# Moving all modulation vectors of a two-layer hybrid network onto the matrix engine

## The chip, the cores and the metric

One NeuronCore of a Trainium2 chip runs the whole network in one launch. The metric is the device time of one launch in microseconds (us), the median of several runs. TensorE multiplies matrices, VectorE (DVE), ScalarE (ACT) and GpSimd (POOL) work element by element, and SyncE (SP) only starts transfers. ACT and POOL start transfers too, each in the order of its own instructions. Every engine takes its instructions strictly in the order in which they stand, and waits on semaphores for the others.

## What is computed

Both layers begin and go on with vectors that come from a conditioning vector `c` (and, for the context rows of layer 0, from `c_ctx`):

```python
def adaln(cond, w, b):                      # w_mod: 2 layers of [1024, 6144], f32
    m = jax.nn.silu(cond) @ w + b
    return jnp.split(m[..., None, :], 6, axis=-1)

def modulate(x, g, shift, scale):
    return rmsnorm(x, g) * (1 + scale) + shift

for layer in range(2):
    sh1, sc1, gt1, sh2, sc2, gt2 = adaln(c, w_mod[layer], b_mod[layer])
    hx = modulate(x, norm_mix_g[layer], sh1, sc1)
    # layer 0: hc = modulate(ctx, ..., csh1, csc1); y = mLSTM and windowed attention of hx, hc
    # layer 1: y = gated MLP over chunks of hx (gMLP)
    x = x + gt1 * y
    x = x + gt2 * ec_moe(modulate(x, norm_ffn_g[layer], sh2, sc2), ...)   # 16 experts
```

`x` has 1024 rows of 1024, `ctx` 256 rows. One layer's weights for these vectors are 25.2 MB. Of layer 0 the first third (sh1, sc1) is needed before anything else, for `c` and for `c_ctx`; the other vectors are needed by the ends of the stages that follow.

## The kernel before, in words

The stages follow one another, by the profiled execution: the row norms and the first modulation (0 to 59 us), the transposes with the modulation and eight projections of the context (to 115), keys and values (to 160), gates and the first query (to 192), the gate arithmetic on DVE (176 to 223), the attention with the other projections filled in (223 to 625), the LSTM scan and the first routing (to 888), the first experts (to 1480), the gMLP (1488 to 2135), the second experts (to the end). Each matrix product is three fp32r products of high and low parts; the weights arrive as `wraw` (one 512 KB transfer for 128 columns), ACT casts them to `wh` (L70) and DVE or POOL subtracts to `wl` (L71).

A modulation piece is 512 of the 6144 columns; four pieces make a batch of 2048. The pieces are made in three ways:

- **Batch 0 of layer 0** (`start`, L199 to L214): eight transfers of 1 MB on SP's queue, two buffers, each followed by four matmuls with an output of two rows (c and c_ctx) by 512 columns (L201). The rows go back through DVE copies (L205) and 16 small transposes (L208). Behind them `transposed` (L161) transposes the normed rows (L167), modulates them on ACT (`hmod`, L172) and splits them into `hH` or `cH` (L175) and `hL` or `cL` (L176, every third on POOL).
- **14 pieces** (`mod_rest`, L608): POOL loads 512 KB (L617, buffers `mw`), scales them by the conditioning (L619) and sums over eight blocks of rows (L621) into a tile that it writes to memory (L625). During the attention `mod_sum` (L627) loads the tile and `mod_reduce` (L634) sums over the partitions on TensorE: four small matmuls into columns (L644), or one into a row (L638).
- **The last six pieces** (`mod_late`, L648): in the gMLP, DVE does the scaling and summing (L656, L658, L661) on tiles `s2k`, and TensorE the reduction (L644, L638). It is called behind each group of columns (L1390, L1391).

In the attention (`attention`, L376 on) each head pair and block gives scores `S` (L386 to L390), softmax pieces `ast` (L396 to L402) and `P` (L413) on DVE and ACT, transposes of P on TensorE (L415), a split into `PH` and `PL` (L417, L418) and the output `O` (L424, L425). Between them `fill` takes steps of a generator of projections (three matmuls of 512 columns a step, L228), `FILLS` says how many. The projections accumulate in the pool `pa`, two PSUM buffers `acc`, one for each half of 512 rows; each half is brought out by ACT (L444 and its like). The final order on each engine is set by a scheduler over the program, so the code's order is not quite the order of an engine.

Of the kernel before, what the change touches and what calls it, by code (L numbers as in the profile page):

```python
# [8 lines left out]
F32 = mybir.dt.float32  # L9
# [9 lines left out]
D = 1024  # L19
# [19 lines left out]
class Kernel:  # L39
# [110 lines left out]
    def normed(self, xt, sm):  # L150

        nc = self.nc
        ss = sm.tile([128, 1], F32, tag="ss", name="ss")
        junk = sm.tile([128, D], BF, tag="junk", name="junk", bufs=1)
        nc.scalar.activation(junk, xt, AF.Square, accum_out=ss)
        nc.vector.tensor_scalar(ss, ss, 1.0 / D, EPS, op0=ALU.mult, op1=ALU.add)
        r = self.rsqrt(sm, ss, 1)
        nc.vector.tensor_scalar(xt, xt, r, None, op0=ALU.mult)

    def transposed(self, xns, pp, sm, gs, sh, hH, hL, c0, f32=None):  # L160
# [3 lines left out]
        for k in range(KD):  # L164
# [3 lines left out]
            if f32 is None:  # L168
                t = sm.tile([128, 512], F32, tag="hmod", name="hmod")[:, :n]
            else:  # L170
                t = f32[:, k, c0:c0 + n]
            nc.scalar.activation(t, ps[:, :n], AF.Identity, bias=sh[:, k:k + 1], scale=gs[:, k:k + 1])  # L172
            if hH is not None:
                h = hH[:, k, c0:c0 + n]
                nc.vector.tensor_copy(h, t)  # L175
# [3 lines left out]
    def start(self):  # L179
        nc, I = self.nc, self.I  # L180
        with ExitStack() as s:
            wp = self.pool(s, "wm", bufs=2)
# [3 lines left out]
            pp = self.pool(s, "pp", bufs=2, space=PSUM)  # L186
# [6 lines left out]
            for xt in xs:  # L193
                self.normed(xt, sm)
            mod = mp.tile([2, 2048], F32, name="mod")
            sil2 = self.sil.rearrange("p (s k) -> p k s", s=2)
            for k in range(KD):
                w = wp.tile([128, 2048], F32, tag="wm", name="wm")
                nc.sync.dma_start(out=w, in_=I["w_mod"][0, k * 128:(k + 1) * 128, 0:2048])  # L199
                for j in range(4):  # L200
                    nc.tensor.matmul(mod[:, j * 512:(j + 1) * 512], sil2[:, k, :], w[:, j * 512:(j + 1) * 512],  # L201
                                     start=(k == 0), stop=(k == KD - 1))
            rows = wp.tile([2, 2048], F32, tag="wm", name="rows")
            for j in range(4):
                nc.vector.tensor_copy(rows[:, j * 512:(j + 1) * 512], mod[:, j * 512:(j + 1) * 512])  # L205
            mt = pp.tile([128, 512], F32, tag="tr", name="tr")
            for j in range(16):
                nc.tensor.transpose(mt[:, 2 * j:2 * j + 2], rows[:, j * 128:(j + 1) * 128], self.ident[0:2, 0:2])  # L208
            mc = self.cp.tile([128, 2, 16], F32, name="mc")
            nc.vector.tensor_tensor(mc, mt[:, 0:32].rearrange("p (j s) -> p s j", s=2),  # L210
                                    self.bcols[:, None, 0:16].to_broadcast([128, 2, 16]), op=ALU.add)
# [5 lines left out]
            self.transposed(xs[0:2], pp, sm, gs[:, 1, :], mc[:, 1, 0:8], self.cH, self.cL, 0)  # L217
            for g in range(2):
                self.transposed(xs[2 + 4 * g:6 + 4 * g], pp, sm, gs[:, 0, :], mc[:, 0, 0:8], self.hH, self.hL, 512 * g)
# [28 lines left out]
    def gates(self, pa, qp, hx, hc):  # L248
# [225 lines left out]
    def layer0_a(self, rings):  # L474
        nc, I = self.nc, self.I
        with ExitStack() as s:
# [87 lines left out]
            for c in range(4):  # L564
                sums = rest[cut[c - 1]:cut[c]] if c else []

                def fill(n):
                    list(itertools.islice(work, n))
                    if n == self.FILLS[2] and sums:
                        self.mod_sum(self.hxp, "hx", pt, [sums.pop(0)])  # L570
# [1074 lines left out]
```

## Time and profile before

| what | value |
|---|---|
| median of 3 runs | 2795.18 us (2794.61 to 2809.98) |
| the profiled execution: its time, its span | 2799.46 us, 2797.7 us |
| PE busy | 2499.7 us, 89% |
| DVE busy | 2061.3 us, 74% |
| ACT busy | 1530.1 us, 55% |
| POOL busy | 921.0 us, 33% |
| chain that ended last | PE 66%, DVE 8%, DMA 3%, issue 3%, ACT 2%, POOL 1% |

The span runs from the first to the last instruction of the profiled execution; the 1.8 us between it and that execution's time lie around it. That execution is 4.3 us longer than the median. The shares are averages over all stages: three quarters of the span are the experts and the gMLP, where TensorE has the work, while the first 223 us are bound by transfers, ACT and DVE in turn.

### The profile page before, as it was taken

The page shows a single profiled execution, that of the slowest core. Times are in us where ns is not written, and L with a number is a line of the kernel's source. Part 1 is how long each engine was busy: PE and PEld are TensorE (multiplying, and loading weights), DVE is VectorE, ACT ScalarE, POOL GpSimd, SP SyncE. Part 2 cuts the span into 40 slices and gives each one's busy share as a digit, 9 for nine tenths or more (in the row PEclk, how much of TensorE's full clock was granted, in tenths as well). Part 3 has the DMA queues.
Part 4 walks back from the last instruction along what each step waited for, and adds up shares of the span by engine and source line. Part 5 has one row for each costly group of instructions (what it writes and reads, how often), then busy time and mean ns, then how long its engine had stood idle before and what let it go on. Part 6 is the DMA issues. An engine that isn't in the chain of part 4 may idle for free.

```text
span 2797.7 us, 34024 instructions
## 1 busy us (share of the span) xinstructions
PE 2499.7 (89%) x12038; PEld 1999.1 (71%) x12038; DVE 2061.3 (74%) x2979; ACT 1530.1 (55%) x2262; POOL 921.0 (33%) x638
## 2 busy tenths in 40 slices
PE   6767888898895999999997999999995999999994
PEld 2656667776774788888775787888884788888773
DVE  4768798767847999999885385035505899999887
ACT  3334344445434888888864224232422788888774
POOL 0688787305531122121003324533451021321102
PEclk9978999999996999999999999999997999999997
DMA  6433434337265999999956423362334999999984
GB/s 242 134 106 114 153 123 156 105 104 269 70 230 234 362 381 382 386 383 385 364 179 208 138 83 115 92 224 76 91 121 184 365 373 388 373 389 382 357 307 150
DMA packets 246465, 648.78 MB, mean 232 GB/s; under 512 B 18572, under 2 KB 84968, under 8 KB 245270
## 3 DMA queue, kind: packets, MB, share of 16 engines
q1 hardware_dynamic: 205584, 528.44, 50.5%
q0 software_dynamic: 22096, 78.72, 10.0%
q10 hardware_dynamic: 18614, 39.44, 4.1%
q8 instruction: 95, 1.56, 0.2%
q14 instruction: 76, 0.62, 0.1%
HBM read 590.85 MB, written 53.07 MB: 230 GB/s over the span
## 4 chain that ended last, share of the span: by engine, by line
PE 66%; DVE 8%; DMA 3%; issue 3%; ACT 2%; POOL 1%; POOLq 0%; ACTq 0%; SPq 0%; DVEq 0%
PE g L1110 13%; PE u L1110 13%; PE d L1110 12%; PE acc L1461 6%; PE acc L1409 6%; PE acc L1385 5%; PE acc L781 2%; PE acc L228 2%; PE tr L1140 1%; DMA wraw<-in_gm_w_in_dram 1%; PE tr L1175 1%; PE acc L1421 1%; PE S L415 1%; PE tr L898 1%; DVE ml L71 1%
## 5 line engine op out<-in xcount | busy, mean ns | idle before, releaser
L71 DVE TENSOR_TENSOR ml<-mraw,mh 128x1024 fp32r<-128x1024 f32 x758 | 884.5, 1222 | 62.8 <-ACT mh L70 62.4
L70 ACT ACTIVATE mh<-mraw 128x1024 fp32r<-128x1024 f32 x758 | 777.3, 1064 | 143.3 <-PE g L1110 71.3
L71 POOL TENSOR_TENSOR wl<-wraw,wh 128x1024 fp32r<-128x1024 f32 (+1 forms) x133 | 257.3, 1945 | 382.8 <-ACT wh L70 378.7
L70 ACT ACTIVATE wh<-wraw 128x1024 fp32r<-128x1024 f32 (+1 forms) x163 | 143.3, 897 | 320.0 <-issue 97.1
L1190 POOL DMA_INDIRECT s_x<-xe,idx x28 | 55.5, 1982 | 662.6 <-ACT hidH L1177 421.5
L1128 POOL DMA_INDIRECT xe<-s_xr,idx x32 | 136.3, 4261 | 278.1 <-ACT mh L70 147.7
L1110 PE MATMUL d<-ml,hidH 128*128 128x512 f32 x512 | 204.5, 399 | 5.0 <-DVE ml L71 4.9
L1110 PE MATMUL g<-mh,xH 128*128 128x512 f32 x512 | 206.9, 404 | 1.4 <-ACT xH L1145 1.4
L1110 PE MATMUL d<-mh,hidH 128*128 128x512 f32 x512 | 205.2, 401 | 3.2 <-DVE o L1187 3.2
L1110 PE MATMUL g<-ml,xH 128*128 128x512 f32 x512 | 205.9, 402 | 1.4 <-DVE ml L71 1.4
L1110 PE MATMUL g<-mh,xL 128*128 128x512 f32 x512 | 205.2, 401 | 0.0
L1110 PE MATMUL u<-ml,xH 128*128 128x512 f32 x512 | 203.4, 397 | 0.2
L1110 PE MATMUL d<-mh,hidL 128*128 128x512 f32 x512 | 203.4, 397 | 0.1
L1110 PE MATMUL u<-mh,xH 128*128 128x512 f32 x512 | 202.2, 395 | 0.0
L1110 PE MATMUL u<-mh,xL 128*128 128x512 f32 x512 | 202.2, 395 | 0.0
L1385 PE MATMUL acc<-wh,h2k 128*128 128x512 f32 x512 | 167.4, 408 | 1.9 <-DVE h2k L1367 1.9
L1409 PE MATMUL acc<-h2k,wh 128*128 128x512 f32 x512 | 161.4, 396 | 0.0
L1461 PE MATMUL acc<-wh,s2k 128*128 128x512 f32 x480 | 152.1, 397 | 0.0
L228 PE MATMUL acc<-hH,wh 128*128 128x512 f32 x368 | 150.8, 410 | 0.0
L228 PE MATMUL acc<-hH,wl 128*128 128x512 f32 x368 | 150.8, 410 | 0.0
L228 PE MATMUL acc<-hL,wh 128*128 128x512 f32 x368 | 150.3, 408 | 0.0
L621 POOL TENSOR_TENSOR macc<-macc,mw 128x512 f32<-128x512 f32 x98 | 143.7, 1466 | 3.7
(462 smaller groups left out, 5572.2 us busy)
## 6 DMA issues: line engine op xcount, KB each, us to landing
mraw<-in_moe_w_down_dram SPq DMA_DIRECT2D x128, 1024.0 KB
mraw<-in_moe_w_gate_dram SPq DMA_DIRECT2D x126, 1024.0 KB
mraw<-in_moe_w_up_dram SPq DMA_DIRECT2D x124, 1024.0 KB
wraw<-in_gm_w_in_dram SPq DMA_DIRECT2D x64, 512.0 KB
mw<-in_w_mod_dram POOLq DMA_DIRECT2D x56, 512.0 KB, 4.9
wraw<-in_gm_w_out_dram SPq DMA_DIRECT2D x32, 512.0 KB
wraw<-in_ab_w_in_dram SPq DMA_DIRECT2D x30, 512.0 KB
s2k<-in_w_mod_dram ACTq DMA_DIRECT2D x48, 256.0 KB
```

Source lines behind the costliest of these rows:

```text
L70: nc.scalar.activation(h, src, AF.Copy)
L71: i = (nc.gpsimd if eng == "pool" else nc.vector).tensor_tensor(l, src, h.bitcast(F32), op=ALU.subtract)
L228: nc.tensor.matmul(acc, a[:, k, :], b[:, k, c0:c0 + n], start=(k == 0 and i == 0), stop=(k == KD - 1 and i == 2))
L415: nc.tensor.transpose(S[i][:, 512 - nl + j * 128:640 - nl + j * 128], P[:, j * 128:(j + 1) * 128], self.ident)
L621: nc.gpsimd.tensor_tensor(acc, acc, wk, op=ALU.add)
L781: nc.tensor.matmul(acc, a[:, k, t * 128:(t + 1) * 128], b[:, k % 2, :], start=(k == 0 and i == 0), stop=(k == 3 and i == 2))
L1110: nc.tensor.matmul(acc[:, sl], a[:, k, :], b[:, sl], start=(k == 0 and i == 0), stop=(k == KD - 1 and i == 2))
L1128: f = nc.gpsimd.indirect_dma_start(out=xe, out_offset=None, in_=self.s_xr[layer], in_offset=bass.IndirectOffsetOnAxis(ap=self.idx[e], axis=0))
L1190: nc.gpsimd.indirect_dma_start(out=self.s_x[layer], out_offset=bass.IndirectOffsetOnAxis(ap=self.idx[e], axis=0), in_=o, in_offset=None, c ...
L1385: nc.tensor.matmul(acc[t], a[k][:, ts], b[:, k2, :], start=(k == 0 and i == 0), stop=(k == KD - 1 and i == 2))
L1409: nc.tensor.matmul(acc, a[:, k, :], b[k], start=(k == 0 and i == 0), stop=(k == KD - 1 and i == 2))
L1461: nc.tensor.matmul(acc, a[:, ts], b[k2], start=(c == 0 and i == 0), stop=(c == 15 and i == 2))
```

## The change

The 24 pieces become six batches of 2048 columns, three of each layer, and all of them go through one generator, `mod_steps`: a step loads 128 rows of the batch (as one transfer of 1 MB in `start`, on SP; as two of 512 KB elsewhere, on POOL's queue) and multiplies them by four matmuls of 32 by 512, each into another 32 partitions of one PSUM bank. The 32 stationary columns `silw` are 16 copies of the two conditionings. `mod_batch` runs the eight steps, copies the bank to `mrows`, adds the bias of the gate rows, and transposes the rest into the columns `modc`. Batches 1 and 2 of layer 0 are stepped by `next(mods)` in the projections of the first 190 us, in a PSUM pool of their own. The three batches of layer 1 are stepped in the attention, at every tenth step of the filled projections, in the pool `pa`, of whose two `acc` buffers one is then held by a batch. `mod_rest`, `mod_sum`, `mod_reduce` and `mod_late` are gone. In `start` the rows are normed in groups and transposed to `xT` by plain copies on ACT, and `modulated` makes `hmod` and the two parts from `xT`, on ACT and DVE alone.

```diff
-    def normed(self, xt, sm):
+    def normed(self, xts, sm):
...
+        for i, xt in enumerate(xts):
+            junk = sm.tile([128, D], BF, tag="junk", name="junk", bufs=1)
+            nc.scalar.activation(junk, xt, AF.Square, accum_out=ss[:, i:i + 1])
...
-            nc.scalar.activation(t, ps[:, :n], AF.Identity, bias=sh[:, k:k + 1], scale=gs[:, k:k + 1])
...
-                (nc.gpsimd if k % 3 == 0 else nc.vector).tensor_tensor(hL[:, k, c0:c0 + n], t, h.bitcast(F32), op=ALU.subtract)
...
+            nc.scalar.activation(xT[:, k, :], ps[:, :n], AF.Copy)
+
+    def modulated(self, xT, sm, gs, sh, hH, hL, c0):
...
+            nc.scalar.activation(t, xT[:, k, :], AF.Identity, bias=sh[:, k:k + 1], scale=gs[:, k:k + 1])
+            nc.vector.tensor_copy(h, t)
+            nc.vector.tensor_tensor(hL[:, k, c0:c0 + n], t, h.bitcast(F32), op=ALU.subtract)
...
-            wp = self.pool(s, "wm", bufs=2)
+            wp = self.pool(s, "wm", bufs=4)
...
+            for g in (xs[0:2], xs[2:6], xs[6:10]):
+                self.normed(g, sm)
+            self.transposed(xs[0:2], pp, xT[:, :, 0:NCTX])
+            for g in range(2):
+                self.transposed(xs[2 + 4 * g:6 + 4 * g], pp, xT[:, :, NCTX + 512 * g:NCTX + 512 * (g + 1)])
+            mod = mod_first()
...
+            lm1 = self.pool(self.cx, "lm1", bufs=2, side="right")
+            ps1 = s.enter_context(ExitStack())
+            pm = self.pool(ps1, "pmod", bufs=1, space=PSUM)
+            mods = itertools.chain(self.mod_batch(lm1, pm, pt, 0, 1), self.mod_batch(lm1, pm, pt, 0, 2))
...
                     self.proj(acc[:, :NCTX], W, hc, 0, NCTX)
+                    next(mods, None)
...
-                self.gates(pa, qp, hx, hc)
+                self.gates(pa, qp, hx, hc, mods)
+                for _ in mods:
+                    pass
+                ps1.close()
                 self.cx.close()
                 self.rp2 = self.pool(c, "rows2")
                 self.gate_math()
...
+            mods = itertools.chain(*(self.mod_batch(lm, pa, pt, 1, b) for b in range(3)))
...
+            def fill(n):
+
+                for _ in itertools.islice(work, n):
+                    if next(steps) % 10 == 9:
+                        next(mods, None)
...
+    def mod_steps(self, pool, acc, layer, b, m, dma):
+
+        nc = self.nc
+        for k in range(KD):
+            ws = []
+            for c in range(0, 2048, m):
+                w = pool.tile([128, m], F32, tag="wm", name="wm")
+                dma.dma_start(out=w, in_=self.I["w_mod"][layer, k * 128:(k + 1) * 128, 2048 * b + c:2048 * b + c + m])
+                ws += [w[:, 512 * j:512 * (j + 1)] for j in range(m // 512)]
+            lhs = self.silw[:, k].rearrange("p a s -> p (a s)")
+            for j in range(4):
+                nc.tensor.matmul(acc[32 * j:32 * j + 32, :], lhs, ws[j], start=(k == 0), stop=(k == KD - 1))
+            yield
+
+    def mod_batch(self, pool, pa, pt, layer, b):
...
+        acc = pa.tile([128, 512], F32, tag="acc", name="acc")
+        yield from self.mod_steps(pool, acc, layer, b, 1024, nc.gpsimd)
+        rows = pool.tile([128, 512], F32, tag="mrows", name="mrows", bufs=1)
+        nc.vector.tensor_copy(rows, acc)
...
+        for t in range(4):
+            nc.tensor.transpose(tr[:, t * 128:(t + 1) * 128], rows[:, t * 128:(t + 1) * 128], self.ident)
...
-                    if 4 * hf + cg < 6:
-                        self.mod_late(lambda: slot(F32), pp.tile([128, 512], F32, tag="tr", name="tr"), 1, 6 + 4 * hf + cg)
```

How the scheduler places this is seen in the order of the engines' instructions. First TensorE at the start of the program (`mod` is the first modulation, `xt` the normed rows, `acc` the first projection). Before:

```order
L201 MATMUL mod<-wm,sil 2x512 x32
L208 MATMUL tr<-cst,rows 128x2 x8
L167 MATMUL tr<-cst,xt 128x128 x2
L208 MATMUL tr<-cst,rows 128x2 x8
L167 MATMUL tr<-cst,xt 128x128 x4
L228 MATMUL acc<-cH,wh 128x256 x2
```

And now:

```order
L123 MATMUL ps<-cst,st 128x124
L124 MATMUL ps<-cst,st_77 128x96
L651 MATMUL mod<-wm,silw 32x512 x32
L170 MATMUL tr<-cst,xt 128x128 x80
L230 MATMUL tr<-cst,rows 128x128 x4
L250 MATMUL acc<-cH,wh 128x256 x2
```

All 80 transposes of rows stand behind the 32 matmuls of the modulation, and all of them ahead of the modulation's own transposes (L230).

Second, TensorE in the attention (`S` scores, `O` outputs, `acc` the filled projections; L250 is the former L228). Before, a reduction of `mod_sum` stands there:

```order
L390 MATMUL S<-kst_661,qst 128x256
L228 MATMUL acc<-hL,wh 128x512
L228 MATMUL acc<-hH,wl 128x512
L424 MATMUL O<-PH,vst_664 128x256
L644 MATMUL tr<-ones,macc 128x1 x4
L228 MATMUL acc<-hH,wh 128x512
```

Now a step of the second batch of layer 1:

```order
L250 MATMUL acc<-hL,wh 128x512
L250 MATMUL acc<-hH,wl 128x512
L651 MATMUL acc<-wm,silw 32x512
L409 LDWEIGHTS identb
L409 MATMUL S<-amask,identb 128x384
L410 MATMUL S<-kst_576,qst 128x384
L411 MATMUL S<-kst_577,qst 128x384
L412 MATMUL S<-kst_576,qst 128x256
L413 MATMUL S<-kst_577,qst 128x256
L651 MATMUL acc<-wm,silw 32x512 x3
L250 MATMUL acc<-hH,wh 128x512
```

The four matmuls of this step stand as one and three; of the 24 steps in the attention 12 are divided so, of the 16 between the start and the attention 10 (as two and two), the others are four in a row.

Third, DVE at the gate arithmetic (`li`, `lf` are the gates, copied out of the projections). Before:

```order
L269 COPY li<-acc 4x512
L269 COPY lf<-acc 4x512
L282 TENSOR_SCALAR lf<-lf,gbias 36x1280
L283 SCALAR_TENSOR_TENSOR gt<-lf 36x1280
L286 SCALAR_TENSOR_TENSOR lf<-lf,gt 36x1280
```

And now:

```order
L292 COPY li<-acc 4x512
L292 COPY lf<-acc 4x512
L305 TENSOR_SCALAR lf<-lf,gbias 36x1280
L660 COPY mrows<-acc 128x512
L666 TENSOR_TENSOR mrows<-mrows,mbias 1x512 x2
L71 TENSOR_TENSOR wl<-wraw,wh 128x1024
L676 TENSOR_TENSOR modc<-tr,bcols 128x8
L885 SCALAR_TENSOR_TENSOR gs_6453<-modc,cols 128x8
L306 SCALAR_TENSOR_TENSOR gt<-lf 36x1280
```

The end of batch 2 now stands between the first and the second instruction of the gate arithmetic (L306 is the former L283).

## Rows read from the trace of the kernel before

**Rows 1.** Windows at the start: busy time by engine, PEclk, DMA share, GB/s.

```profile
0.00:10.00 10.00, 0.60 (x2) 0.29 (x2) 1.04 (x10) 1.50 (x2) 1.06 (x8) 1.00 0.55 186
10.00:20.00 10.00, 8.88 (x16) 1.46 (x16) 0.34 (x3) 0.00 (x0) 0.00 (x0) 1.00 1.04 387
20.00:30.00 10.00, 2.13 (x3) 0.34 (x4) 7.04 (x36) 5.23 (x8) 0.00 (x0) 0.74 1.02 424
```

**Rows 2.** Timeline of PE at the start: start us, us, instruction, count, idle before.

```profile
42.09 3.60 PE L201 MATMUL mod<-wm,sil 128*2 128x512 f32 x8 [0.38 <-DMA wm<-in_w_mod_dram]
60.25 0.78 PE L228 MATMUL acc<-cH,wh 128*128 128x256 f32 x2
```

**Rows 3.** By line: duration ns min/median/max, first and last start us.

```profile
L155 ACT ACTIVATE junk<-xt x10: 1040/1057/1059, 21.5 to 52.8; 128x1024 bf16<-128x1024 f32 x10
L172 ACT ACTIVATE hmod<-tr,mc,gs x24: 555/773/782, 59.3 to 90.3; 128x512 f32<-128x512 f32 x16, 128x256 f32<-128x256 f32 x8
L175 DVE CAST hH<-hmod x16: 411/420/1444, 66.7 to 93.1; 128x512 fp32r<-128x512 f32 x16
L176 DVE TENSOR_TENSOR hL<-hmod,hH x10: 676/680/693, 68.8 to 93.9; 128x512 fp32r<-128x512 f32 x10
L497 ACT ACTIVATE cpad<-acc x4: 367/373/375, 69.2 to 99.3; 128x256 f32<-128x256 f32 x4
L518 ACT ACTIVATE rx<-acc x2: 599/599/599, 114.8 to 120.3; 128x512 f32<-128x512 f32 x2
```

**Rows 4.** DMA issues from 90 to 115 us: KB each, median us to landing.

```profile
mw<-in_w_mod_dram POOLq DMA_DIRECT2D x4, 512.0 KB, 4.4
```

**Rows 5.** By line: DVE around the gate arithmetic, columns as in the rows 3.

```profile
L269 DVE COPY lf<-acc x3: 427/693/694, 162.3 to 174.2; 4x512 f32<-4x512 f32 x2, 4x256 f32<-4x256 f32 x1
L283 DVE SCALAR_TENSOR_TENSOR gt<-lf x1: 2789/2789/2789, 176.1 to 176.1; 36x1280 f32<-36x1280 f32 x1
L293 DVE SCALAR_TENSOR_TENSOR li<-li,gbias,gt x1: 1544/1544/1544, 190.3 to 190.3; 36x1280 f32<-36x1280 f32 x1
L396 DVE TENSOR_REDUCE ast<-S x64: 672/812/826, 223.1 to 608.7; 128x1 f32<-128x640 f32 x48, 128x1 f32<-128x512 f32 x16
```

**Rows 6.** Timeline of PE behind the k projection, columns as in the rows 2.

```profile
149.66 0.58 PE L228 MATMUL acc<-cH,wh 128*128 128x256 f32 x1 [15.43 <-ACT rx L532]
```

**Rows 7.** Timeline of PE, two projection matmuls in a row.

```profile
618.64 0.39 PE L228 MATMUL acc<-hL,wh 128*128 128x512 f32 x1
618.87 0.39 PE L228 MATMUL acc<-hH,wl 128*128 128x512 f32 x1
```

**Rows 8.** Windows of the attention, columns as in the rows 1.

```profile
225.00:325.00 100.00, 84.63 (x439) 68.16 (x438) 86.06 (x132) 41.73 (x85) 79.97 (x76) 0.94 0.44 139
425.00:525.00 100.00, 87.14 (x463) 70.25 (x464) 84.02 (x131) 39.73 (x83) 74.38 (x71) 0.95 0.43 135
525.00:625.00 100.00, 96.37 (x531) 78.10 (x530) 67.67 (x150) 45.43 (x98) 1.46 (x2) 0.98 0.31 103
```

**Rows 9.** PE groups, 225 to 626: busy us, mean ns, idle before, releasers.

```profile
L415 PE MATMUL S<-cst,P 128*128 128x128 f32 x304 | 48.3, 293 | 40.6 <-DVE P L413 26.0 <-DVE ast L402 10.1 <-DVE va L456 2.3
L644 PE MATMUL tr<-ones,macc 128*128 128x1 f32 x64 | 7.7, 239 | 1.2 <-DMA macc<-s_acc 1.2
L638 PE MATMUL tr<-macc,ones 128*1 128x512 f32 x12 | 6.1, 590 | 1.6 <-DMA macc<-s_acc 1.6
```

**Rows 10.** The same of DVE, 225 to 525 us.

```profile
L401 DVE TENSOR_TENSOR ast<-ast 128x1 f32<-128x1 f32 x46 | 25.8, 562 | 9.0 <-ACT P L400 8.6
```

**Rows 11.** The same of DVE, 525 to 612 us.

```profile
L401 DVE TENSOR_TENSOR ast<-ast 128x1 f32<-128x1 f32 x18 | 2.7, 156 | 6.2 <-ACT P L400 6.0
```

**Rows 12.** The same of PE in the gMLP, 1488 to 2135 us.

```profile
L644 PE MATMUL tr<-ones,s2k 128*128 128x1 f32 x32 | 5.7, 300 | 17.4 <-DVE s2k L661 17.4
```

**Rows 13.** Windows in the gMLP, columns as in the rows 1.

```profile
1540.00:1545.00 5.00, 5.00 (x15) 3.88 (x15) 0.00 (x0) 0.19 (x1) 0.00 (x0) 0.63 0.01 3
1630.00:1635.00 5.00, 5.00 (x24) 4.89 (x24) 3.18 (x8) 0.00 (x0) 0.00 (x0) 0.50 0.00 0
```

More of the change, by code (lines that the diff above doesn't have):

```diff
@@ L192, in start @@
                 xs.append(xt)
[L193 to L202, printed above, removed]
@@ L203, in start, with mod_first @@
-            rows = wp.tile([2, 2048], F32, tag="wm", name="rows")
+            def mod_first():
+                mod = mp.tile([128, 512], F32, name="mod")
+                for _ in self.mod_steps(wp, mod, 0, 0, 2048, nc.sync):
+                    pass
+                return mod
+            for g in (xs[0:2], xs[2:6], xs[6:10]):
+                self.normed(g, sm)
+            self.transposed(xs[0:2], pp, xT[:, :, 0:NCTX])
+            for g in range(2):
+                self.transposed(xs[2 + 4 * g:6 + 4 * g], pp, xT[:, :, NCTX + 512 * g:NCTX + 512 * (g + 1)])
@@ L204, in start @@
+            mod = mod_first()
+            rows = sm.tile([128, 512], F32, tag="rows", name="rows", bufs=1)
+            nc.vector.tensor_copy(rows, mod)
+            mt = pp.tile([128, 512], F32, tag="tr", name="tr")
             for j in range(4):
[L205 to L208, printed above, removed]
+                nc.tensor.transpose(mt[:, j * 128:(j + 1) * 128], rows[:, j * 128:(j + 1) * 128], self.ident)
@@ L209, in start @@
             mc = self.cp.tile([128, 2, 16], F32, name="mc")
[L210 to L211 removed]
+            for s_ in range(2):
+                nc.vector.tensor_tensor(mc[:, s_, :].rearrange("p (j t) -> p j t", j=4),
+                                        mt.rearrange("p (t j r) -> p j t r", t=4, j=4)[:, :, :, s_],
+                                        self.bcols[:, 0:16].rearrange("p (j t) -> p j t", j=4), op=ALU.add)
@@ L553, in layer0_a @@
             self.hxp = self.pool(rings, "hxp", side="right")
+            lm = self.pool(s, "lm", bufs=2)
             hd = self.pool(s, "head")
             self.pss = self.pool(s, "pss", bufs=2, space=PSUM)
-            rest = [(0, j) for j in range(4, 12)] + [(1, j) for j in range(6)]
-            cut = (0, 4, 9, 14, 14)
             Q = []
@@ L561, in layer0_a @@
             Qs = [Q, [], [], []]
+            mods = itertools.chain(*(self.mod_batch(lm, pa, pt, 1, b) for b in range(3)))
             work = itertools.chain(*(itertools.chain(self.query(pa, qp, c + 1, hx, Qs[c + 1]) if c < 3 else (),
                                                      self.head_in(pa, hd, c, hx), self.head_gate(c) if c < 3 else ()) for c in range(4)))
-            for c in range(4):
[L565 to L570, printed above, removed]
+            steps = itertools.count()
+            def fill(n):
+                for _ in itertools.islice(work, n):
+                    if next(steps) % 10 == 9:
+                        next(mods, None)
+            for c in range(4):
                 self.attention(hd, c, Qs[c], fill)
-                if c == 3:
-                    for _ in work:
-                        pass
-                self.mod_rest(lm, rest[cut[c]:cut[c + 1]])
+            for _ in itertools.chain(work, mods):
+                pass
         self.dump("colU", self.colU)
@@ L627, in mod_sum @@
-    def mod_sum(self, pool, tag, pp, pieces):
-        nc = self.nc
-        for layer, pc in pieces:
-            acc = pool.tile([128, 512], F32, tag=tag, name="macc", bufs=2)
-            nc.sync.dma_start(out=acc, in_=self.s_acc[layer, pc])
-            self.mod_reduce(acc, pp.tile([128, 512], F32, tag="tr", name="tr"), layer, pc)
-    def mod_reduce(self, acc, ps, layer, pc):
-        nc = self.nc
-        which = pc // 2
-        if which in (2, 5):
-            nc.tensor.matmul(ps[0:1, :], self.ones[:, 0:1], acc, start=True, stop=True)
-            nc.vector.tensor_copy(acc[0:1, :], ps[0:1, :])
-            i = 2 * layer + (which == 5)
-            nc.sync.dma_start(out=self.s_gt[i:i + 1, 512 * (pc % 2):512 * (pc % 2) + 512], in_=acc[0:1, :])
-        else:
-            for j in range(4):
-                nc.tensor.matmul(ps[:, j:j + 1], acc[:, j * 128:(j + 1) * 128], self.ones[:, 0:1], start=True, stop=True)
-            nc.vector.tensor_copy(self.modc[:, layer, 4 * pc:4 * pc + 4], ps[:, 0:4])
```

108 lines of the change are left out of this document (52 added, 56 removed).

## The prediction

> **What bounds the kernel now.** I read the windows by stage first, then the groups and waits of TensorE (PE) in the stages that the change touches, then the single rows behind each wait. The experts, the LSTM and the routing hold no modulation work, and I leave them at what they are. Four stages are touched.
>
> In the start, transfers set the pace: 186, 387 and 424 GB/s in the first three windows [rows 1], with PE waiting for each modulation block, whose four matmuls take 3.60 us as eight records [rows 2]. The first modulated rows leave ACT at 59.3 and the last at 91 [rows 3]; the first projection begins at 60.25 [rows 2]. Up to 223 us a chain follows: k projection done at 120.3 [rows 3], PE idle for 15.43 us until the rotated keys come [rows 6], the gates' last copy at 174.2, DVE's gate arithmetic from 176.1 until the attention's first reduction at 223.1 [rows 5]. In the attention PE is 85 to 87% busy and DVE 84 to 86% for three of four windows (two are shown), and PE waits for DVE's softmax [rows 7, 8]. In the gMLP PE is the bound, and stops four times for the late pieces' sums on DVE, 17.4 us [rows 12].
>
> **The unknown, s.** No row shows matmuls in column groups. Call s the PE time of a step, four matmuls of 32 by 512. Lower bound 0.90: all four side by side, each as long as one matmul's two records (3.60/4) [rows 2]. Upper bound 3.60: no overlap. I take the middle model. A float32 matmul is two records here, and both use the same group, so they can't lie side by side; taken in order, the first of the next group can lie beside the second of this one. Four matmuls are then five slots instead of eight. A slot is 0.43: the 3.60 less one record's duration, 0.59 as of the same shape in [rows 9], over seven. That makes 2.15. A step that is cut into two parts costs one slot more, 2.58, or with full overlap 1.8. By the order of the instructions 10 of 16 steps ahead of the attention and 12 of its 24 are cut, so the mean of s is 2.38 with half overlap and 1.38 with full; without any it stays 3.6.
>
> **Start, first 90 us.** Despite the intention, all 80 row transposes stand behind the modulation on PE, and ACT's first weight cast waits for weights that are queued on SP behind 8 MB of modulation. By 30 us 10.0 MB have come (1.9 + 3.9 + 4.2) [rows 1]; 14.2 MB are needed (rows, modulation, two weight blocks), the rest at about 400 GB/s: 41 us, modulation done at 44. Four buffers instead of two keep the queue full, so I add no wait. Then ACT has its chain: two or three weight casts at about the 1.06 of a square of the same size, five squares at an estimated 1.25 (1.06 and the read-out of the sum), 8 copies at 0.37 and about 16 at 0.57, taken a little under the 0.60 of their like [rows 3]: 20.4 us, and 1.6 for the last transposes and the vectors. First modulated rows at 66 instead of 59.3. The pass over them is DVE's: 16 × (0.42 + 0.68) for the rows, about 4.4 for the context at half the size [rows 3], with overlap 20, and three weight subtractions of twice that size, 1.3 each by it. It ends near 90 instead of 94.6 (93.9 and 0.68), and ACT's last part 1.5 sooner, at 88.5.
>
> **Keys, 90 to 150.** The pool of the moved loads reuses memory that this pass reads, so the first half block starts at 88.5 and lands at 93 (4.4 for 512 KB [rows 4]). With two buffers each step waits for the load that its predecessor's matmuls released: 4.6 + s/2 a step. The eight steps of batch 1 stand in PE's order between the context projections and the end of the k projection, which is thus done at 93 + s + 7 × (4.6 + s/2) + s/2 and 3.7 of projection, 129 + 5s, instead of 120.3: **+8.7 + 5s**. Behind it the rotation of the keys no longer shares with POOL: a fifth of the 15.43 [rows 6], **−3**.
>
> **Gates, 150 to 223.** One step more on the chain, s. Then the gate arithmetic waits for batch 2's end, which stands between its first two DVE instructions: query 0's 48 matmuls at 0.23 [rows 7] are 10.9, with copy, biases and transposes 12.3, and two more steps, instead of 1.9 behind the last gate copy [rows 5]: **+10.4 + 3s** with the one before. What it hides behind now, the query, ran beside the arithmetic before. Free of POOL the 47.0 us of DVE shrink: one instruction of 36x1280 took 2.79 us with POOL at work, another 1.54 [rows 5], but not all suffer so; I take a fifth, **−9.4** (bounds 0 and 21). Together +6.7 + 9s, counting s, 5s and 3s.
>
> **Attention.** POOL's 220 multiplications and sums go. With POOL at 74 to 80 us in 100, tiny sums on DVE took 562 ns; with POOL idle 156 [rows 10, 11]. PE got 439 to 463 instructions in 100 us in three windows, 1360 in all, and 531 in the last [rows 8]. All 1891 at 5.31 a microsecond are 356 us instead of 400: **−44**. The reductions go: 7.7 + 6.1 [rows 9], **−14**. The steps come: **+24s**, PE being the engine that is filled. One accumulator of two is held by a batch, so a projection half waits until ACT has brought the last one out; of 36 such places seven or eight have nothing between on PE, at 0.6 [rows 3] and as much queueing on ACT: **+8**. DVE waits and PE's waits for P (26.0 [rows 9]) are in the −44.
>
> **gMLP.** The four waits, 17.4, and 32 small matmuls, 5.7 [rows 12], go, and the half clock behind two of the waits: 0.63 over 5 us and 0.50 over 5 us [rows 13], 4.4: **−27**. DVE's 48 multiply-adds go with them; DVE isn't the bound there.
>
> **The sum**: 6.7 − 44 − 14 + 8 − 27 = −70 + 33s. It breaks even at s = 2.1. With 2.38: **+8**. From the profiled 2799.5 that is 2807.5; that execution is 4.3 above the median, so against the runs 2803.
>
> TensorE: Matmul & The Clock Gate of the Trainium skill, section Part 3: Packing small matmuls, gives 3.07 times the speed for four row groups and 2.38 for three column groups; no run here shows it. By 3.07 an uncut step would be an estimated 1.2 us and the sum near −20, which is rival B. Against the change speaks the page TensorEngine Tiling (Array Packing), section Key Properties: a change of tiling mode drains the engine, and each step changes it at least twice. The trace shows how deep the pipe is, 0.39 us of duration at a spacing of 0.23 [rows 7]; at 0.16 a drain, some 62 parts of steps with two each would add an estimated 20 us at most, and I hold that for inside the range.
>
> **Rivals.** A is the forecast, half overlap, 2803, own range 2777 to 2829 (the fifth taken for POOL's share, −44 between −25 and −55, +8 up to 30). Chance 0.40.
>
> B, full overlap: s = 1.38, −70 + 46 = −24, 2771. For it: the four groups are different columns of the array and different outputs. Against it: the two records of one matmul must follow each other. It has nearly the weight of A, since the trace speaks for neither directly; I put A first because the two records do show in it. Chance 0.37.
>
> C, slower: no overlap at all, s = 3.6, −70 + 119 = +49, 2844. It decides from s = 2.95 (+28). For it: in every pair of rows here the second record starts a full slot behind the first, as in [rows 7]. Chance 0.15.
>
> D, slower by the accumulator: if the 36 halves each wait 2 us on ACT's queue, 72 instead of 8, it is 2867 with A's s; it decides from 0.8 us each (8 + 20 over 36). Against it: the fill steps lie between attention matmuls, which need no accumulator. Chance 0.08.
>
> The range 2752 to 2848 leaves out most of D, half of C and B's lower end, about 0.17. A measurement of this kernel can tell about 1% (28 us). Faster by that: half of B and a little of A, 0.22. Slower: C, D and a quarter of A, 0.33. Within: 0.45.
>
> **What would show it.** The rows of L651 in the attention tell s directly: first to last start of four. First modulated rows near 66, k projection done near 141, the gate arithmetic's second instruction some 20 us behind the gates' last copy, DVE's tiny sums at 156 ns all through the attention, no wait in the gMLP for L661's like. I am wrong if s is under 1.5, if PE waits for the accumulator in the attention, or if loads of modulation (4.4 us before) take longer beside the weights.

## The result, and the profile after

The changed kernel takes 2779.72 us (median of 8 runs, 2778.42 to 2784.49); the kernel before, beside it, 2806.81 (2792.69 to 2811.13). The ratio of comparable runs is 0.9923, with a 95% interval of 0.9905 to 0.9942: 0.8% faster, some 22 us. The medians lie 27 us apart; the eight runs of the kernel before spread over 18 us. The two profiled spans, 2797.7 and 2777.1, are 20.6 apart. I had forecast 8 us slower. The time lies in the range and inside the 1% that I called no change, but on the other side.

From the page of the changed kernel, the busy times of the engines:

```profile
PE 2518.2 (91%) x12254; PEld 1977.9 (71%) x12254; DVE 1933.1 (70%) x2848; ACT 1540.6 (55%) x2286; POOL 617.4 (22%) x417
```

TensorE (PE) has 18.5 us more to do than before, DVE 128 less and POOL 304 less. Where the time went is read from the first and last starts of lines that end a stage. First the same lines as in [rows 3, 5] in the changed kernel (duration ns min/median/max, first and last start us): first modulated rows, end of the k projection, gates' last copy, the gate arithmetic's second instruction, the attention's first reduction.

```profile
L180 ACT ACTIVATE hmod<-xT,mc,gs x24: 586/803/821, 63.8 to 88.8; 128x512 f32<-128x512 f32 x16, 128x256 f32<-128x256 f32 x8
L547 ACT ACTIVATE rx<-acc x2: 597/598/600, 137.6 to 146.0; 128x512 f32<-128x512 f32 x2
L292 DVE COPY lf<-acc x3: 426/693/695, 185.5 to 199.9; 4x512 f32<-4x512 f32 x2, 4x256 f32<-4x256 f32 x1
L306 DVE SCALAR_TENSOR_TENSOR gt<-lf x1: 1476/1476/1476, 216.6 to 216.6; 36x1280 f32<-36x1280 f32 x1
L419 DVE TENSOR_REDUCE ast<-S x64: 673/820/826, 251.3 to 623.7; 128x1 f32<-128x640 f32 x48, 128x1 f32<-128x512 f32 x16
```

| stage, us of the span | before | after | moved | forecast |
|---|---|---|---|---|
| to the attention's first reduction | 223.1 | 251.3 | +28.2 | +28 (6.7 + 9s) |
| attention, to the LSTM's first product | 410.9 | 397.6 | −13.3 | +7 (−50 + 24s) |
| LSTM and first routing | 253.4 | 253.5 | 0 | 0 |
| first experts | 600.8 | 598.7 | −2 | 0 |
| gMLP, to its last projection | 640.7 | 609.6 | −31.1 | −27 |
| second experts | 668.8 | 666.4 | −2 | 0 |

The lines that bound the attention and the gMLP, before and after (first products of the LSTM and of the gMLP, and the gMLP's last projection):

```profile
L725 PE MATMUL num<-va,nP x128: 273/275/585, 634.0 to 752.8; 128*128 128x130 f32 x128
L742 PE MATMUL num<-va,nP x128: 272/275/585, 648.9 to 768.1; 128*128 128x130 f32 x128
L1385 PE MATMUL acc<-wh,h2k x512: 389/397/792, 1488.2 to 1923.8; 128*128 128x512 f32 x171
L1402 PE MATMUL acc<-wh,h2k x512: 391/397/796, 1501.1 to 1905.5; 128*128 128x512 f32 x171
L1461 PE MATMUL acc<-wlate,s2k x48: 387/396/486, 2109.5 to 2128.9; 128*128 128x512 f32 x48
L1476 PE MATMUL acc<-wlate,s2k x48: 387/396/485, 2091.3 to 2110.7; 128*128 128x512 f32 x48
```

So the forecast fails in the attention, by 20 of the 29 us between forecast and spans. What it rested on there is one number, s. Timeline of PE in the changed kernel, a step of four in a row and one that is cut (start us, us, instruction, count):

```profile
269.18 0.40 PE L250 MATMUL acc<-hH,wl 128*128 128x512 f32 x1
269.51 1.06 PE L651 MATMUL acc<-wm,silw 128*32 128x512 f32 x8
270.50 0.50 PE L250 MATMUL acc<-hH,wh 128*128 128x512 f32 x1
```

```profile
386.51 0.39 PE L250 MATMUL acc<-hH,wl 128*128 128x512 f32 x1
386.82 1.05 PE L651 MATMUL acc<-wm,silw 128*32 128x512 f32 x2
387.80 0.34 PE L409 MATMUL S<-amask,identb 128*128 128x384 bf16 x1
...
388.64 1.06 PE L651 MATMUL acc<-wm,silw 128*32 128x512 f32 x6
389.63 0.50 PE L250 MATMUL acc<-hH,wh 128*128 128x512 f32 x1
```

All eight records of the whole step lie in 1.06 us, and the next matmul starts 0.99 behind the step's first record. In the records themselves the four first ones start 6 to 7 ns apart, and each matmul's second record starts 453 ns behind its first. The pairs did not stand in line, as my model had them: the order is all four first halves, then all four second ones. One matmul alone (386.82, two records) costs just as much, 0.98, and so does a part of three, 0.99. Between two projection matmuls, which start 0.23 apart without a step [rows 7], the whole step takes 1.32 (269.18 to 270.50), so it adds 1.09. The whole lot in the attention, with the idle time before it (groups of PE from 251 to 649 us: busy us, mean ns | idle before):

```profile
L651 PE MATMUL acc<-wm,silw 128*32 128x512 f32 x192 | 41.3, 624 | 9.1 <-DMA wm<-in_w_mod_dram 9.1
```

1.72 us of PE a step in the mean of whole and cut ones, where I had 2.38, and 9.1 us of waits for loads that I had not put there. Most of these waits, 6.6 us, belong to the first step, whose loads land late; at a granted clock of 0.50 that step also takes 3.8 us of PE.

The other terms, in the same views as before. The windows of the attention [rows 8], one of them:

```profile
351.00:451.00 100.00, 98.04 (x537) 71.91 (x536) 71.81 (x140) 45.03 (x92) 7.95 (x14) 1.00 0.41 132
```

The tiny sums on DVE while the steps run [rows 10, 11]:

```profile
L424 DVE TENSOR_TENSOR ast<-ast 128x1 f32<-128x1 f32 x50 | 7.7, 156 | 13.1 <-ACT P L423 12.7
```

They take 156 ns in this window (252 to 552 us) and 158 in the rest of the attention. PE's waits between 252 and 650 (us in total, times, longest):

```profile
PE acc L651 <- DMA wm<-in_w_mod_dram: 9.1, 3, 5.5
PE acc L250 <- ACT pad L467: 1.9, 3, 0.9
PE S L438 <- DVE P L436: 1.9, 7, 0.3
```

The 26.0 us of waits for P [rows 9] are 1.9. The wait for the accumulator's eviction, for which I had 8, is about 2. In the gMLP no wait for a modulation sum is left [rows 12].

Ahead of the attention PE waits for something that the forecast did not have (waits from 8 to 260 us):

```profile
PE acc L250 <- ACT cpad L524: 16.9, 1, 16.9
PE acc L651 <- DMA wm<-in_w_mod_dram: 16.1, 12, 5.5
PE tr L365 <- ACT cs L340: 17.7, 1, 17.7
```

```profile
90.14 0.58 PE L250 MATMUL acc<-cH,wh 128*128 128x256 f32 x1 [16.88 <-ACT cpad L524]
```

```profile
L524 ACT ACTIVATE cpad<-acc x4: 367/376/386, 89.7 to 122.6; 128x256 f32<-128x256 f32 x4
```

After the first two context projections PE stands still until 90.14, since both accumulators are full and their evictions stand behind the modulation of all the rows on ACT: the first is at 89.7, where it was at 69.2 before [rows 3]. Before, that modulation came in pieces, between the transposes. The 17.7 stand behind the gate arithmetic, where PE waited before too (12.6 and 4.2). The longest wait for a load, 5.5, ends in the attention and is one of the 9.1 above; ahead of the attention they are 10.6, by the group of PE from 90 to 215 us, which also has what the 16 steps there cost, 33.4:

```profile
L651 PE MATMUL acc<-wm,silw 128*32 128x512 f32 x128 | 33.4, 646 | 10.6 <-DMA wm<-in_w_mod_dram 10.6
```

### The profile page after: what moved, and what is told of

Same layout as the page of the kernel before. It is cut to its first block, busy times and chain, and to the rows that moved or that the text cites. A ratio compares the mean times of both kernels' runs of the same rounds, so it can differ in the third digit from the quotient of the medians.

```text
span 2777.1 us, 33996 instructions
## 1 busy us (share of the span) xinstructions
PE 2518.2 (91%) x12254; PEld 1977.9 (71%) x12254; DVE 1933.1 (70%) x2848; ACT 1540.6 (55%) x2286; POOL 617.4 (22%) x417
## 4 chain that ended last, share of the span: by engine, by line
PE 76%; DVE 9%; DMA 7%; issue 4%; ACT 4%; POOL 1%; ACTq 0%; POOLq 0%; SPq 0%; DVEq 0%
PE g L1127 13%; PE u L1127 13%; PE d L1127 12%; PE acc L1402 6%; PE acc L250 6%; PE acc L1476 6%; PE acc L1424 6%; DMA wm<-in_w_mod_dram 3%; PE acc L798 2%; PE acc L651 2%; PE S L438 1%; PE tr L1157 1%; DVE s2k L1418 1%; PE tr L1192 1%; PE O L447 1%
## 5 line engine op out<-in xcount | busy, mean ns | idle before, releaser
L70 ACT ACTIVATE mh<-mraw 128x1024 fp32r<-128x1024 f32 x758 | 776.9, 1063 | 141.4 <-PE g L1127 69.2
L1207 POOL DMA_INDIRECT s_x<-xe,idx x28 | 45.1, 1610 | 675.6 <-ACT hidH L1194 447.1
L647 POOL DMA_DIRECT2D wm<-in_w_mod_dram x80 | 43.8, 549 | 494.8 <-PE acc L651 364.1
L250 PE MATMUL acc<-hH,wh 128*128 128x512 f32 x368 | 150.4, 409 | 2.3 <-ACT pad L467 1.9
L250 PE MATMUL acc<-hH,wl 128*128 128x512 f32 x368 | 146.3, 398 | 0.0
L250 PE MATMUL acc<-hL,wh 128*128 128x512 f32 x368 | 146.0, 397 | 0.0
```

Of the source, the lines that this page charges most:

```text
L70: nc.scalar.activation(h, src, AF.Copy)
L250: nc.tensor.matmul(acc, a[:, k, :], b[:, k, c0:c0 + n], start=(k == 0 and i == 0), stop=(k == KD - 1 and i == 2))
L647: dma.dma_start(out=w, in_=self.I["w_mod"][layer, k * 128:(k + 1) * 128, 2048 * b + c:2048 * b + c + m])
L1207: nc.gpsimd.indirect_dma_start(out=self.s_x[layer], out_offset=bass.IndirectOffsetOnAxis(ap=self.idx[e], axis=0), in_=o, in_offset=None, c ...
```

## The experiments

The stage times below are read as in the table. Of the first four runs there is one execution each.

### All steps in one column group

```diff
-                nc.tensor.matmul(acc[32 * j:32 * j + 32, :], lhs, ws[j], start=(k == 0), stop=(k == KD - 1))
+                nc.tensor.matmul(acc[32 * j:32 * j + 32, :] if k == 0 else acc[0:32, :], lhs, ws[j],
+                                 start=(k == 0), stop=(k == 0 and j > 0) or (k == KD - 1 and j == 3))
```

> The changed kernel, but from the second block of rows of each batch on all four matmuls of a step go to the first column group and add up in its 32 partitions (so the modulation vectors are wrong; all loads and the number of matmuls stay). Theory: the four groups of a step run side by side, about 1.1 us of TensorE for a step of four in a row and 2.15 for a step cut in two, and TensorE is the engine that sets the attention; then the eight records of a step take 3.4 to 3.6 us one behind the other, the attention (first score reduction to first LSTM product, 397.6 us in the changed kernel) grows by 35 to 45 us, and the 28 us before it by 8 to 25 more. In all 45 to 65 us slower than the change. Rival: the steps lie beside waits, TensorE is not the bound there; then the attention grows by under 15 us.

It took 2838.96 us (span 2837.1): 60.0 of span more than the change. The attention lasts 431.6 instead of 397.6, +34, a little under what I expected, and begins at 273.8, 22.5 later. The groups of PE in its attention (274 to 705 us):

```profile
L651 PE MATMUL acc<-wm,silw 128*32 128x512 f32 x192 | 85.7, 622 | 5.8 <-DMA wm<-in_w_mod_dram 5.8
```

A step of four in a row in this run:

```profile
382.13 3.62 PE L651 MATMUL acc<-wm,silw 128*32 128x512 f32 x8
385.68 0.50 PE L250 MATMUL acc<-hH,wh 128*128 128x512 f32 x1
```

The same 192 records take 85.7 us of PE instead of 41.3, 3.6 a step with the first steps still side by side; the step shown takes 3.55 to the next matmul, where the four groups take 0.99. So the groups do overlap, PE's time there is the kernel's time for the most part (34 of 44), and this is rival C's kernel: 2839 against the 2844 worked out for it.

### The steps left out, with the accumulator held or given back

```diff
         for k in range(KD):
+            if layer == 1 and k:
+                yield
+                continue
...
```

> The changed kernel, but the three batches of layer 1 make only their first step of eight (seven eighths of the sum left out, with their loads); each batch still holds its accumulator over the same eight places in the order. Theory: a step costs 1.1 or, cut, 2.15 us of the attention, so 21 steps less take 30 to 37 us off its 397.6. Rival: the attention is bound by DVE's softmax, and under 12 us go.

2737.69 us; the attention lasts 355.4, so 21 steps were worth 42.2, 2.0 each. The same group in this run (251 to 607 us):

```profile
L654 PE MATMUL acc<-wm,silw 128*32 128x512 f32 x24 | 7.0, 756 | 6.6 <-DMA wm<-in_w_mod_dram 6.6
```

Of the 42.2, 34 are PE's own (41.3 − 7.0), 2.5 the load waits (6.6 are left); the remaining 5 I can't place. That is more than the 30 to 37 expected. The other form ends a batch behind its one step (`range(1 if layer == 1 else KD)`):

> As the run before, but a batch ends right after its one step and gives its accumulator back. Theory of the prediction: a projection that has one accumulator of two waits for its eviction, in sum about 8 us, which go here beyond the run before. Rival: the waits fall where TensorE has other work, and the two runs agree within 3 us. Against 36 waits of 2 us it would be 60 us faster than the run before.

2756.75 us: the attention lasts 370.7, 15 us *longer* with the accumulator free. Neither theory had that. Windows of the two runs at the same time (us, then busy us by engine, PEclk, DMA share, GB/s), held and free:

```profile
575.00:600.00 25.00, 23.83 (x130) 19.20 (x128) 11.57 (x26) 7.82 (x16) 0.59 (x2) 1.00 0.61 209
```

```profile
575.00:600.00 25.00, 13.98 (x69) 11.67 (x67) 13.44 (x33) 9.19 (x22) 0.00 (x0) 0.71 0.21 67
```

With two accumulators all the way, the scheduler has put the projections earlier, and none stands in this stretch of the attention, where the held form has 70 of their records; PE is busy for 14.0 of 25 us in it, and its granted clock is 0.71 in the mean of the two levels, against 1.00. So giving the buffer back moved the order as well, and this pair does not show the price of the held buffer alone. PE's waits do: 1.9 us in the changed kernel, 0.7 in the held form, none in the free one. Whether the order alone makes the 15 us was not tried.

### The kernel before without POOL's and DVE's sums

```diff
-                nc.gpsimd.tensor_scalar(wk if k else acc, wk, self.sil[:, k:k + 1], 0.0, op0=ALU.mult, op1=ALU.add)
-                if k:
-                    nc.gpsimd.tensor_tensor(acc, acc, wk, op=ALU.add)
+                if k % 2 == 0:
+                    nc.gpsimd.tensor_scalar(acc[:, 0:8] if k else acc, wk[:, 0:8] if k else wk, ...)
...
-            if k:
-                nc.vector.scalar_tensor_tensor(acc, w, self.sil[:, k:k + 1], acc, op0=ALU.mult, op1=ALU.add)
-            else:
+            if k == 0:
```

> The kernel before, with POOL's multiplications and sums of the 14 pieces cut to eight columns at every second block, and DVE's sums of the six late pieces cut to the first block (modulation vectors wrong; all loads, writes and the reductions on TensorE stay). Theory: DVE is slow beside a busy POOL; then the attention (410.9 us) loses 35 to 50 us, the gate arithmetic 9 to 13, and the gMLP (1488 to 2030) 15 to 25 for the waits on the late sums. Rival: the gain of the change in the attention came from the reductions that left TensorE alone (14 us) and not from POOL; then the attention loses under 15 us here.

2718.95 us, against 2795.97 for the kernel before beside it. The attention lasts 366.6, −44.3, and begins at 201.4; from the gates' last copy to it are 38.9 instead of 48.9; the gMLP loses 16.9. A window, and the tiny sums again (301 to 501 us):

```profile
301.00:401.00 100.00, 97.66 (x558) 81.03 (x558) 77.74 (x160) 49.40 (x103) 7.45 (x12) 1.00 0.33 101
```

```profile
L401 DVE TENSOR_TENSOR ast<-ast 128x1 f32<-128x1 f32 x38 | 5.9, 155 | 9.6 <-ACT P L400 9.1
```

558 instructions of PE in 100 us against 439 to 463 [rows 8]. The term of −44 for POOL's share of the attention holds to the microsecond, partly by luck; a busy POOL was what made DVE's tiny sums slow. Not all of DVE suffers. In the kernel before, from 225 to 525 us:

```profile
L397 DVE SCALAR_TENSOR_TENSOR ast<-ast,nsink 128x1 f32<-128x1 f32 x45 | 23.1, 514 | 0.4
L402 DVE RECIPROCAL ast<-ast 128x1 f32<-128x1 f32 x46 | 7.3, 160 | 0.8
L413 DVE TENSOR_SCALAR P<-P,ast 128x640 f32<-128x640 f32 x36 | 27.5, 767 | 0.6
```

The first takes 154 ns with POOL idle and the third 553, but the reciprocal takes 160 either way. By their means (562 for 156, 514 for 154, 767 for 553) the two slow ones and the tiny sums cost DVE 43 us more over the 300 us, about what the attention loses without POOL's sums.

In all the run is 77 us shorter than the kernel before, by one execution each, which is about what the sums on POOL and DVE cost there. The change has got back some 22 of these, and the fastest version below some 50.

### The start: buffers, batch 2, queues, order

The next four were timed beside the kernel before (2802.85). First `bufs=4` for `lm1`:

> The changed kernel with four buffers instead of two for the half blocks of batches 1 and 2. Theory: ahead of the attention TensorE waits for these loads (16.1 us between 94 and 175, the step period of 6.4 us is a landing of 4.8 and the rest of a cycle), since each load waits for the matmuls on its predecessor; with four buffers the attention begins 8 to 16 us sooner than at 251.3, and the whole is as much shorter than the change (2779.7). Rival: the first load, behind the modulation of the rows, and the eviction wait of 16.9 us set this stage; then under 4 us.

2759.30 us, ratio to the kernel before 0.9844 (0.9807 to 0.9881). The attention begins at 233.0, 18 sooner: a little more than the theory gave, and the gate arithmetic starts 8 us behind the gates' last copy instead of 16.7. PE's waits for these loads go only from 10.6 to 6.3, and the eviction wait of 16.9 stays; the gates' last copy comes at 189.0 instead of 199.9. The 16.1 us of load waits in the expectation hold the 5.5 that end in the attention. Then batch 2 in the attention:

```diff
-            mods = itertools.chain(self.mod_batch(lm1, pm, pt, 0, 1), self.mod_batch(lm1, pm, pt, 0, 2))
+            mods = self.mod_batch(lm1, pm, pt, 0, 1)
...
-                    if next(steps) % 10 == 9:
+                    if next(steps) % 7 == 6:
```

> The changed kernel with batch 2 of layer 0 stepped in the attention, ahead of layer 1's batches, at every seventh filled step instead of every tenth. Theory: the gate arithmetic waits for batch 2's end (16.7 us behind the gates' last copy against 1.9 before the change), so the attention begins 13 to 20 us sooner than at 251.3, and grows by eight steps of 2.0 us, 16; in sum between 5 us faster and 5 slower than the change. Rival: the gate arithmetic isn't what the attention's start waits for; then it begins under 5 us sooner and the whole is 10 to 16 us slower.

2768.91 us, 0.9888 (0.9848 to 0.9928). The gate arithmetic (L306) now starts 1.6 behind the last copy's start, the attention at 227.5, 24 sooner, and it lasts 410.5, 13 longer (1.6 a step). The theory has the sign of both and misses both ranges: 24 for 13 to 20, and 13 for 16, so that the whole is 11 us faster than the change and not within 5 of it. Of the 24, 15 are the wait of the gate arithmetic; the other 9 come since the gates' last copy itself is at 191.0 instead of 199.9. Then the first modulation on POOL's queue (`nc.gpsimd` for `nc.sync`):

> The changed kernel with the first modulation's eight transfers on POOL's queue, so that the first weights on SP's queue no longer stand behind them and ACT's first weight cast doesn't hold back its squares. Theory: ACT's chain behind that cast (20 us from 43) sets the first modulated rows at 63.8; now they come at 55 to 59 and the attention begins 4 to 8 us sooner. Rival: the transfers as a whole set it, the modulation lands later by the weights that now go beside it, and nothing is gained (under 2 us either way).

2777.86 us, 0.9914 (0.9886 to 0.9943), no different from the change.

```profile
L180 ACT ACTIVATE hmod<-xT,mc,gs x24: 587/806/819, 62.5 to 86.5; 128x512 f32<-128x512 f32 x16, 128x256 f32<-128x256 f32 x8
```

First modulated rows at 62.5 instead of 63.8, and the attention at 248.3, 3 sooner, where 4 to 8 were expected: the rival is nearer. Its last modulation matmuls start at 47.7 instead of 41.8; what ACT no longer holds up, the transfers do. Then the context projections among the rows (`ctx_heads` is the loop over `hd` of `layer0_a`, `modulated` a generator that yields behind each k):

```diff
+            list(itertools.islice(xmod, 2))
...
-            for g in range(2):
-                c0 = NCTX + 512 * g
-                self.modulated(xT[:, :, c0:c0 + 512], sm, gs[:, 0, :], mc[:, 0, 0:8], self.hH, self.hL, 512 * g)
...
+            xmod = itertools.chain(*(self.modulated(xT[:, :, NCTX + 512 * g:NCTX + 512 * g + 512], sm, gs[:, 0, :], mc[:, 0, 0:8],
+                                                    self.hH, self.hL, 512 * g) for g in range(2)))
+            self.ctx_heads(self.pool(late, "ctxp", bufs=2), self.pool(late, "ptr0", bufs=2, space=PSUM), xmod)
...
```

> The run with batch 2 in the attention, and also: the eight context projections stand in the program among the modulation of the 1024 rows (two of its sixteen pieces behind each eviction), ahead of batch 1's steps, which go to keys, values and gates. Theory: TensorE's idle 16.9 us from 73 to 90 came from the evictions standing behind all modulated rows on ACT, and its waits for loads from the pool that reuses the rows' memory; both go, the k projection is done at 115 to 128 instead of 146, and the kernel is 12 to 30 us faster than the run with batch 2 alone. Rival: DVE's pass over the rows, which ends near 90, sets the k projection, and under 8 us are gained on that run.

2757.45 us, 0.9840 (0.9803 to 0.9877). The k projection is done at 121.8, near the 120.3 of [rows 3], and PE's wait for the eviction is

```profile
PE acc L282 <- ACT cpad L197: 1.8, 1, 1.8
```

instead of 16.9. That part of the theory holds; the whole is 11.5 us under the run with batch 2 alone, short of the 12 to 30: the gate arithmetic is now 9 behind the last copy, as batch 1 has moved there.

### Versions that put these together

> The run with the context projections among the rows and batch 2 in the attention, with four buffers for batch 1 and the first modulation's transfers on POOL's queue. Theory: batch 1 ends sooner, and the gate arithmetic starts 2 to 4 us behind the gates' last copy instead of 9; the attention begins at 203 to 210 instead of 214.6, and the kernel takes 2744 to 2753 us. Rival: the loads of batch 1 are bound by their start behind the modulated rows, and four buffers bring under 3 us.

2756.84 us, 0.9848 (0.9823 to 0.9873): not faster than the run before it, and above the 2753 expected. The gate arithmetic starts 3 behind the last copy and the attention at 210.6, both as expected but for the last microsecond, and the attention lasts 412.4; the 4 us that it begins sooner are lost by small amounts in three later stages. Its rival, that four buffers bring under 3 us, holds for the whole and not for the attention's start.

> The changed kernel with the context projections among the modulation of the rows, and the pools of batches 1 and 2 (four buffers) opened ahead of the rows' memory, so that their loads need not wait for it; all 16 steps stay ahead of the attention and 24 in it. Theory: neither the eviction wait (16.9) nor the loads' chain is left, the gate arithmetic isn't behind batch 2, and the attention keeps its 24 steps: k projection done at 120 to 130, the attention begins at 200 to 215 and lasts 393 to 398, in all 2728 to 2745 us. Rival: the early loads take their bandwidth from the first modulation and the rows; then the first modulated rows come 5 us later or more, and it is not faster than the run before this one.

2753.81 us, 0.9835 (0.9812 to 0.9859). That is no faster than the run before it beyond the noise, and above the 2745 expected. The rival's condition came true: the first modulated rows at 79.9, 16 us late, since the loads of batch 1 go beside the first modulation, whose matmuls alternate with batch 1's on PE. The k projection is done at 139.3 and the attention begins at 223.2, both well behind what was expected. What the attention saved (393.7 long, against 412.4 with batch 2 in it) paid for it.

> The changed kernel with the context projections among the modulation of the rows, and one pool of two buffers for the loads of all five later batches, which reuses the memory of the untransposed rows and the first modulation; so the loads start when the rows are transposed, neither beside the first modulation (the run with early pools lost 16 us there) nor behind the modulated rows, and the gate arithmetic doesn't wait for the pool's end. Theory: first modulated rows at 63 to 65, k projection done at 120 to 130, gate arithmetic within 4 us of the gates' last copy, attention from 203 to 213 for 393 to 400 us; in all 2733 to 2748 us, the fastest here. Rival: with two buffers each load still waits for its predecessor's matmuls; then the k projection is done at 138 or later and the whole takes over 2752.

2753.07 us, 0.9816 (0.9781 to 0.9850), the lowest median, not to be told from the run before it, and under the changed kernel's interval. It is above the 2748 expected, where the rival had it, but the rival's sign (the k projection at 138 or later) did not come: it is done at 129.2. First rows at 63.0, gate arithmetic 1.6 behind the last copy, the attention 396.7 long; but it begins at 220.4, not by 213. The wait for batch 2 has only moved by one instruction: its copy now stands behind the second instruction of the gate arithmetic, and DVE waits there.

```profile
188.75 0.69 DVE L669 COPY mrows<-acc 128x512 f32<-128x512 f32 x1 [8.18 <-PE acc L660]
```

8.0 us of PE's waits for the two buffers' loads are left ahead of the attention and 7.9 in it. From LSTM to first experts it takes 261.7 in this execution, 8 us more than in the change; I have no cause for it.

## Why the prediction was wrong

**The unknown, s: failed.** The step was "taken in order, the first of the next group can lie beside the second of this one", five slots for four matmuls, 2.15, and a cut worth one slot more. The trace has two slots for any number of groups from one to four: 0.99 whole, 0.98 and 0.99 for the two parts of a cut step, 1.97 together. The bound 0.90 was nearly the value, and rival B's 1.38 for the mean is 1.72 by busy time, the slow first step included. With 1.7 the sum −70 + 33s is −14, on the side that was measured. The one-group run ties the price to the overlap and not to the order of the work. My own sign of being wrong, s under 1.5, was set too low: what turns the sum is the break-even of 2.1, and 1.72 lies below it.

**The loads in the attention, at nothing: failed.** The steps wait 9.1 us for them there. They land in 4.6 us ahead of the attention and 4.8 in it, in the median, where I had 4.4.

**The accumulator, +8: failed.** PE's waits for it are some 2 us. Rival D, which made it 72, is out.

**POOL's share, −44: right**, shown by the kernel before without POOL's sums (−44.3). With the reductions' −14, their own load waits of 2.8 [rows 9], which I left out, the steps' 41.3, 9.1 of load waits and 2 for the accumulator the attention's terms give −8, against −13.3 measured; about 5 us stay unassigned.

**Start, +28: right in sum by luck, wrong in parts.** First modulated rows 63.8 for 66 and their last 88.8 for 88.5 were good. Behind them I had 9 × 2.38 for the steps' own time. By busy time the 16 steps took 2.1 each (33.4 us), more than in the attention, since halves of a load that came late also split steps that stand in a row, and some ran at half clock (the first took 3.1, at a granted clock of 0.51). Two waits came on top: 16.9 us for evictions behind ACT's modulation, which I did not see although the order of ACT shows it, and loads with a step period of 6.4 us instead of 4.6 and half an s, 5.8. So the k projection was done at 146, where I had 141. PE's wait of 15.43 for the rotated keys [rows 6], of which I let 3 go, is not there any more. The gate arithmetic started 16.7 behind the gates' last copy, where I had 12.3 and two steps, 17, and its own gain free of POOL was larger: 34.7 from its second instruction to the attention for 47.0, −12.3 for −9.4. That instruction alone took 1.48 us for 2.79.

**gMLP, −27: right**, −31. Of it 17 come without DVE's sums alone, as the run without these sums shows.

**Not foreseen:** the two expert stages are 2 us shorter each. They have the same code in every run here and vary from 598.7 to 602.5 and from 664.4 to 669.7, so this may be chance.

The rules that I weighed: of packed matmuls the Trainium skill (TensorE: Matmul & The Clock Gate, Part 3: Packing small matmuls) gives 3.07 times for four row groups; four column groups here go 3.6 times as fast (3.55 one behind the other in the one-group run, by 0.99). The drain at a change of mode, which the Trainium skill states without a size (TensorEngine Tiling (Array Packing), Key Properties), is visible at most as 0.1 us on either side of a part: 0.33 from the last projection matmul instead of 0.23, and 0.54 for the last slot instead of 0.43. The second is inside the 0.99, the first is the 0.10 that makes it 1.09.

## What to carry to other kernels

Work that an idle engine does for nothing may be paid for by its neighbour: POOL's sums cost the attention 44 us, by slowing DVE, nearly as much as layer 1's steps cost it on the busiest engine (50 with their load waits). When a stage is split in two passes, look at what now stands behind the whole of the first pass on each engine: here two small evictions did, and PE stood for 17 us. A wait that is taken from one instruction can come back at the next: look for it in the whole chain, not only where it stood. And a sum whose sign hangs on one price that no row shows should be told as its break-even: here 2.1 us a step, between bounds of 0.9 and 3.6.

## What the hardware showed

Four float32 matmuls of 32 columns in four column groups take as long as one (0.99 against 0.98 us), each as two records, first halves together, second halves together; in one column group they take 3.55. A cut of the four over other work therefore costs the whole price twice. Four buffers of 512 KB loads instead of two took 18 us off a stage in which the loads had been only 10.6 us of PE's listed waits. With POOL 74 to 80% busy a 128x1 sum on DVE took 562 ns instead of 156, and a 128x1 reciprocal 160 as ever.
